# One-core hybrid decoder trunk: attention steps of the first two token tiles with scheduling priority, and the search's scratch tiles in a longer-lived pool

## The chip, the cores and the metric

The kernel runs on 1 core of one Trainium2 chip. The metric is the device time of one execution in microseconds (us), lower is better. Before the change it is 1992.75 us, the median of 3 runs (1991.83 to 1993.22).

## The reference

Two decoder layers over 512 tokens of width 1024, in float32. In each layer one projection `h @ w_in` feeds four branches: A, a gated convolution; B, sparse attention; C, a gated linear recurrence (HGRN2); M, cross-attention into 256 memory tokens. Each branch is lifted to width 1024, gated per channel, and summed; one output projection and a SwiGLU feed-forward network follow. The change touches branch B alone:

```python
def one_block(args):                       # a block of 128 queries
    qb, iqb, iwb, qpos = args
    rel = jax.nn.relu(jnp.einsum('bthd,bsd->bths', iqb, ik) * idx_scale)
    score = jnp.einsum('bths,bth->bts', rel, iwb).astype(jnp.float32)
    causal = key_pos[None, :] <= qpos[:, None]
    score = jnp.where(causal[None], score, -jnp.inf)
    _, sel = lax.top_k(score, topk)        # topk = 128 keys per query
    ...
    logits = jnp.einsum('bthd,btkd->bthk', qb, k_sel).astype(jnp.float32) * att_scale
    logits = jnp.where(valid[:, :, None, :], logits, -jnp.inf)
    p = jax.nn.softmax(logits, axis=-1).astype(v.dtype)
    return jnp.einsum('bthk,btkd->bthd', p, v_sel)
```

An indexer scores every key for every query, the 128 best keys are kept, and eight heads of 64 channels attend to these keys with one shared key and value.

## The kernel before, in words

**Weights.** Each weight chunk of 512 KB is loaded by a DMA on SyncE's queue into one of 4 buffers `w_raw`. ScalarE rounds it to a high part `w_hi` (L100, by the helper `A`), VectorE subtracts to get the low part `w_lo` (L257); there are 3 buffers of each. A product is then three matmuls per k tile: high by high (L324), high by low (L325 or L327), low by high (the other). GpSimd sums feed-forward weights by DMAs of its own meanwhile.

**The attention branch, per layer.** `select(t)` is the search for token tile t (128 queries, keys 0 to (t+1)·128): eight index heads of scores, then 16 rounds, each a MAX of the 8 largest (L1008) and a MATCH_REPLACE that strikes them out (L1009), on VectorE; last a bias is made from what was struck out (L1012, `biases[t]`). Tile 0 needs no search, its bias is the causal mask. `attend(t)` is the attention of tile t, in two halves of four heads. For each head two matmuls, the dots (L841, L842), go into a buffer `at` of PSUM, of which there are 2; one VectorE instruction (L857) reads `at`, adds the bias, writes `prob` and takes the extremum; ScalarE makes the exponential and its sum; VectorE takes the reciprocal (L860); ScalarE multiplies by it (the "copy"). TensorE transposes the four `prob` (L871) into a buffer `tr`, ScalarE copies them to `pt`, and after both halves matmuls with the values and the write to `y_b` (L890) follow.

**What stands beside it.** The searches are woven with `lift(3)`, the lift and gate of branch M. Then the pool `att` opens, and `attend` of tiles 0 to 3 is woven with `values(hv)` (the value projection of branch C, results `hv`) and with `lift(0)` (the gates and lift of branch A: products `mm`, then VectorE's gate operations L222, L665, L684, L685).

**What sets the order.** A scheduler orders the instructions of each engine by priority, which is the place in the program unless `tc.high_priority(offset=n)` moves it n forward; the weights' splits and some evictions have an offset of AHEAD = 3000. Each engine then runs its list strictly in that order. Pools hand out memory in a stack: `dsa` holds q, k, v and biases of branch B and lives through attend; `idx` is nested in it, holds the index heads' tensors, the score and the top-k scratch `m8`, and ends before the attention. A tile that takes memory of a closed pool waits for the tiles that stood there.

The functions that the change touches:

Of the kernel before, what the change touches and what calls it, by code (L numbers as in the profile page):

```python
# [12 lines left out]
F32 = mybir.dt.float32  # L13
# [8 lines left out]
P = 128  # L22
S = 512
# [18 lines left out]
NONC = -2.0e38  # L42
OFF = -1.0e30
AHEAD = 3000
EARLY = ["mmbmcmcbmmmsccbmscmbscmbsbbss", "mnmbmcmcbmmmsccbmscmbscmbsbbss"]
MM_BUFS = 3
TR_BUFS = 3
# [24 lines left out]
def hybrid_trunk(ctx: ExitStack, tc: tile.TileContext, x, mem, positions, norm_mix, w_in, conv_w,  # L72
# [20 lines left out]
    def A(dst, src, func, **kw):  # L93
        name = tables.get(func)
        if name is not None and name != table["set"]:
            load = act.preload_act_table_set(name)
            for u in table["users"]:
                tc.add_manual_dep(load.ins, u.name, order, reason="table set")
            table.update(set=name, load=load.ins, users=[])
        i = act.activation(dst, src, func, **kw)  # L100
        if name is not None:
            tc.add_manual_dep(i.ins, table["load"].name, order, reason="table set")
            table["users"].append(i.ins)
        return i
# [4 lines left out]
    def at_ps():  # L109
        return pat.tile([P, 512], F32, name="at", bufs=AT_BUFS)  # L110

    def tr_ps():
        return pat.tile([P, 512], F32, name="tr", bufs=TR_BUFS)
# [101 lines left out]
    def small(n, name="small", bufs=12):  # L215
        return consts.tile([P, 8], F32, name=name, bufs=bufs)[:, :n]
# [11 lines left out]
    class Chunk:  # L228
        def __init__(self, src, kt, n):
            self.kt, self.step = kt, min(kt, 1024 // n)  # L230
            self.parts = []
            for k in range(0, kt, self.step):
# [11 lines left out]
                else:  # L244
                    for g in range(2):
                        nc.sync.dma_start(raw.rearrange("p k (g c) -> p k g c", g=2)[:, :, g, :], src[:, k:e, g, :])
                with tc.high_priority(offset=AHEAD):
                    if len(raw_loads) == 1:
# [37 lines left out]
    def features(w, a, js, k0=0, kt=None, pss=None, made=None, late_lo=False):  # L286

        kt = w.kt if kt is None else kt
        pss = [mm_ps() for _ in js] if pss is None else pss
        runs = [(part, ks) for part in range(2) for ks, _, _ in w.parts] if late_lo else [(None, ks) for ks, _, _ in w.parts]  # L290
        for part, ks in runs:
            for j, ps in zip(js, pss):
                for k in ks:
                    last = mm3(ps, w.tile(k, j), pair(a, k0 + k), k0 + k == 0, k0 + k == kt - 1, part=part)[-1]
            if made is not None and (ks[-1] == w.kt - 1 or not late_lo):
                made.append(last)
        return pss
# [232 lines left out]
    def mem_kv(l):  # L530
# [21 lines left out]
        for t, ps in enumerate(products(0)):  # L552
            ku = sp.tile([P, 4, P], F32, name="ku_w", bufs=2)
            with tc.high_priority(offset=AHEAD):
                A(ku.rearrange("p a b -> p (a b)"), ps, AF.Copy)
# [23 lines left out]
        for t, ps in enumerate(products(512)):  # L579
            ps = ps.rearrange("p (h d) -> p h d", d=P)  # L580
            hi, lo = (kv[:, :, 1, e, t * P:(t + 1) * P] for e in range(2))
            with tc.high_priority(offset=AHEAD):
                A(hi, ps, AF.Copy, scale=mem_r[:, t:t + 1])
# [50 lines left out]
    def mixer(l, h, norms, cm):  # L634
# [19 lines left out]
        def lift(n, y, merged, last=None):  # L654
            def gates(m):
# [7 lines left out]
                for g, ps in zip(gs, features(gw, h, (0, 1), made=made, late_lo=made is not None)):  # L663
                    with tc.high_priority(offset=AHEAD):
                        dve.tensor_mul(g, ps, r_b)  # L665
# [5 lines left out]
            for m in range(0, KD, 2):  # L671
# [6 lines left out]
                for i in range(2):  # L678
                    g, pl = gs[i], pls[i]
                    with tc.high_priority(offset=AHEAD):  # L680
                        if n == 3:
# [33 lines left out]
        def conv_branch(y):  # L715
            for c2 in range(2):
                us = [gate_tile(), gate_tile()]
                w = wchunk(w_in[l][:, C_AX + c2 * 256:C_AX + (c2 + 1) * 256], KD, 256)
                for u, ps in zip(us, features(w, h, (0, 1))):
                    (dve if l or c2 else pool).memset(u[:, 0:2], 0.0)  # L720
                    with tc.high_priority(offset=AHEAD):
                        i = dve.tensor_mul(u[:, 2:], ps, r_b)
# [109 lines left out]
        with pool_("dsa") as dp:  # L832
# [8 lines left out]
                return [pe.matmul(ps, q[:, hh, s], k[0][:, :n], start=True, stop=False),  # L841
                        pe.matmul(ps, q[:, hh, s], k[1][:, :n], start=False, stop=True)]  # L842

            def attend(t, dp2, y_b):
                n = (t + 1) * P
                s = slice(t * P, (t + 1) * P)
                pts = []
                for q in range(2):
                    probs = []
                    for i in range(4):  # L850
                        ps = at_ps()[:, :n]
                        two = dots(ps, qS, kS, 4 * q + i, t, n)
                        if t == 0 and q + i // 2:
                            first_dots.extend(two)
                        p = dp2.tile([P, S], F32, name="prob", bufs=PR_BUFS)[:, :n]
                        mx, sm = small(1), small(1)
                        dve.tensor_tensor_reduce(out=p, in0=ps, in1=biases[t], scale=-1.0, scalar=-OFF * 4,  # L857
                                                 op0=OP.add, op1=OP.min, accum_out=mx)
                        A(p, p, AF.Exp, bias=mx, scale=-1.0, accum_out=sm)
                        dve.reciprocal(sm, sm)  # L860
                        copy = A(p, p, AF.Copy, scale=sm)
                        if l and t == 0 and q == 0 and i // 2:
                            first_probs.append(copy)
                        probs.append(p)
                    pt = dp2.tile([P, NT, S], F32, name="pt", bufs=PT_BUFS)
                    copied = []
                    for b in range(t + 1):
                        pp = tr_ps()
                        for e in range(2):
                            for i in range(2):  # L870
                                turn = pe.transpose(pp[:, (2 * e + i) * P:(2 * e + i + 1) * P],  # L871
                                                    probs[2 * i + e][:, b * P:(b + 1) * P], ident)
                        copied.append(A(pt[:, b, :], pp, AF.Copy))
                    pts.append(pt)
                    if q == 0:
                        yield
                pv = tr_ps()
                for q, pt in enumerate(pts):
                    c = slice(q * 2 * P, (q + 1) * 2 * P)
                    for b in range(t + 1):  # L880
                        for e in range(2):
                            i = pe.matmul(pv[e * HD:(e + 1) * HD, c], vt[:, b, :], pt[:, b, e * 2 * P:(e + 1) * 2 * P],  # L882
                                          start=b == 0, stop=b == t)
                            if q == 0 and b == 0:
                                tc.add_manual_dep(i.ins, turn.ins.name, order, reason="turns first")
                                tc.add_manual_dep(i.ins, copied[max(t - 1, 0)].ins.name, sync, reason="values together")
                pv = pv.rearrange("p (a b) -> p a b", b=P)
                hi, lo = (x[:, :, s] for x in y_b)
                A(hi, pv, AF.Copy)
                dve.tensor_sub(lo, pv, f(hi))  # L890
                yield

            with pool_("idx") as ip:
                iqS = ip.tile([P, 8, S], F32R, name="iqS")
# [95 lines left out]

                def select(t):
                    n = (t + 1) * P
                    score = ip.tile([P, S], F32, name="score", bufs=1)[:, :n]
                    for hh in range(8):
                        ps = at_ps()[:, :n]
                        dots(ps, iqS, ikS, hh, t, n)
                        rel = wide()[:, :n]
                        A(rel, ps, AF.Relu, scale=HD ** -0.5)
                        if hh == 0:
                            dve.tensor_scalar(score, rel, iw[:, t, 0:1], 0.0, op0=OP.mult, op1=OP.add)  # L1000
                        else:
                            dve.scalar_tensor_tensor(score, rel, iw[:, t, hh:hh + 1], score, op0=OP.mult,
                                                     op1=OP.add)
                    dve.copy_predicated(score[:, t * P:], future, neg.to_broadcast([P, P]))
                    yield
                    for i in range(TOPK // 8):
                        m8 = ip.tile([P, 16], F32, name="m8", bufs=2)[:, :8]
                        dve.max(m8, score)  # L1008
                        dve.match_replace(score, m8, score, REPL)  # L1009
                        if i % 4 == 3:  # L1010
                            yield
                    dve.tensor_scalar(biases[t], score, REPL, OFF, op0=OP.not_equal, op1=OP.mult)  # L1012
# [20 lines left out]
                with pool_("memat", "left") as mp:  # L1033
                    sel = chain(select(1), select(2), select(3))
                    script(EARLY[l], {"b": projections(), "c": conv_branch(y_a), "m": mem_branch(mp, y_m), "s": sel, "n": late_norm()})
                mgp = cm.enter_context(pool_("mgp", "left"))
                merged = mgp.tile([P, KD, S], F32, name="merged")
                weave(lift(3, y_m, merged), sel, R1)
            y_b = new_y()
# [644 lines left out]
```

## Time and profile before

| | |
|---|---|
| median of 3 runs | 1992.75 us (1991.83 to 1993.22) |
| profiled execution, its own time | 1991.71 us |
| its span | 1989.7 us |
| granted TensorE clock, mean | 0.994 |
| TensorE busy | 1959.2 us (98%) |
| VectorE busy | 1468.1 us (74%) |
| ScalarE busy | 1171.7 us (59%) |
| GpSimd busy | 236.1 us (12%) |

The profile is one execution. PE is TensorE's matmuls, PEld its weight loads, DVE is VectorE, ACT ScalarE, POOL GpSimd, SP SyncE. A row of a timeline gives start, length, engine, line, operation and tile, and in brackets how long the engine was idle before it and which instruction ended that. PEclk is the clock that TensorE was granted, 1.00 being full. Matmuls are pipelined: a row's length is longer than the distance to the next row, so the distance of starts is what a matmul costs.

### The profile page before, as it was taken

The page shows a single profiled execution, that of the slowest core. Times are in us where ns is not written, and L with a number is a line of the kernel's source. Part 1 is how long each engine was busy: PE and PEld are TensorE (multiplying, and loading weights), DVE is VectorE, ACT ScalarE, POOL GpSimd, SP SyncE. Part 2 cuts the span into 40 slices and gives each one's busy share as a digit, 9 for nine tenths or more (in the row PEclk, how much of TensorE's full clock was granted, in tenths as well). Part 3 has the DMA queues.
Part 4 walks back from the last instruction along what each step waited for, and adds up shares of the span by engine and source line. Part 5 has one row for each costly group of instructions (what it writes and reads, how often), then busy time and mean ns, then how long its engine had stood idle before and what let it go on. Part 6 is the DMA issues. An engine that isn't in the chain of part 4 may idle for free.

```text
span 1989.7 us, 26286 instructions
## 1 busy us (share of the span) xinstructions
PE 1959.2 (98%) x9495; PEld 1626.9 (82%) x9495; DVE 1468.1 (74%) x2569; ACT 1171.7 (59%) x1950; POOL 236.1 (12%) x288
## 2 busy tenths in 40 slices
PE   9999997999999999999999999989999999999999
PEld 8888886878888888888888888768888888888887
DVE  7865898658776677776876589975678667767777
ACT  6744563866665466645654547368567656646554
POOL 1011111111111111100011111111111111111000
PEclk9999998999999999999999999989999999999999
DMA  8677776667677888876677766666677788898664
GB/s 301 206 182 174 164 168 139 161 146 179 169 195 197 236 237 245 252 213 187 201 216 174 179 157 161 147 165 155 158 170 170 202 201 239 252 270 249 201 189 138
DMA packets 220178, 385.22 MB, mean 194 GB/s; under 512 B 13194, under 2 KB 114128, under 8 KB 219792
## 3 DMA queue, kind: packets, MB, share of 16 engines
q1 hardware_dynamic: 160960, 244.16, 39.4%
q0 software_dynamic: 52192, 132.81, 33.1%
q10 hardware_dynamic: 6896, 6.58, 1.0%
q8 instruction: 74, 1.21, 0.3%
q14 instruction: 56, 0.46, 0.1%
HBM read 368.81 MB, written 140.51 MB: 256 GB/s over the span
## 4 chain that ended last, share of the span: by engine, by line
PE 96%; DVE 3%; ACT 0%; issue 0%; DVEq 0%; ACTq 0%
PE mm L327 23%; PE mm L324 23%; PE mm L325 23%; PE at L324 4%; PE at L325 4%; PE at L327 4%; PE tr L324 2%; PE tr L327 2%; PE tr L325 2%; DVE score L1009 1%; DVE m L1008 1%; PE tr L871 1%; PE tr L882 1%; PE tr L1576 1%; PE at L841 1%; PE at L842 1%
## 5 line engine op out<-in xcount | busy, mean ns | idle before, releaser
L100 ACT ACTIVATE w_hi<-w_raw 128x1024 fp32r<-128x1024 f32 (+1 forms) x435 | 457.5, 1054 | 360.0 <-PE mm L325 121.4
L324 PE MATMUL mm<-h_hi,w_hi 128*128 128x512 f32 x960 | 377.0, 394 | 0.6 <-DVE zg L1075 0.6
L325 PE MATMUL mm<-h_lo,w_hi 128*128 128x512 f32 x960 | 376.6, 392 | 0.0
L327 PE MATMUL mm<-h_hi,w_lo 128*128 128x512 f32 x960 | 375.9, 398 | 0.0
L257 DVE TENSOR_TENSOR w_lo<-w_raw,w_hi 128x1024 fp32r<-128x1024 f32 (+1 forms) x224 | 272.1, 1217 | 111.4 <-ACT w_hi L100 108.7
L1287 DVE TENSOR_TENSOR w_lo<-w_raw,w_hi 128x1024 fp32r<-128x1024 f32 x211 | 256.4, 1218 | 130.0 <-ACT w_hi L100 129.2
L1302 POOL DMA_DIRECT2D up_sums<-in_ffn_w_up_dram x120 | 121.5, 1012 | 827.7 <-DMA up_sums<-in_ffn_w_up_dram 531.5
L327 PEld LDWEIGHTS mm<-h_hi,w_lo 128*128 128x128 f32 x960 | 183.1, 191 | 37.2 <-issue 0.2
L324 PEld LDWEIGHTS mm<-h_hi,w_hi 128*128 128x128 f32 x960 | 180.4, 188 | 36.6 <-issue 1.0
L325 PEld LDWEIGHTS mm<-h_lo,w_hi 128*128 128x128 f32 x960 | 180.4, 188 | 36.4 <-issue 0.2
L327 PE MATMUL mm<-w_hi,h_lo 128*128 128x512 f32 (+2 forms) x408 | 152.0, 373 | 0.0
L325 PE MATMUL mm<-w_lo,h_hi 128*128 128x512 f32 (+2 forms) x408 | 151.7, 372 | 0.3 <-DVE w_lo L257 0.3
L324 PE MATMUL mm<-w_hi,h_hi 128*128 128x512 f32 (+2 forms) x408 | 145.6, 372 | 0.0
L1302 POOL DMA_DIRECT2D w_sums<-in_ffn_w_down_dram x66 | 62.3, 944 | 339.7 <-DMA w_sums<-in_ffn_w_down_dram 192.2
L100 ACT ACTIVATE prob<-prob,small 128x128 f32<-128x128 f32 (+3 forms) x128 | 68.8, 554 | 49.1 <-DVE small L857 39.9
L325 PEld LDWEIGHTS mm<-w_lo,h_hi 128*128 128x128 f32 x408 | 76.8, 188 | 12.8 <-DVE w_lo L257 0.6
L324 PEld LDWEIGHTS mm<-w_hi,h_hi 128*128 128x128 f32 x408 | 76.8, 188 | 12.3 <-ACT w_hi L100 0.2
L327 PEld LDWEIGHTS mm<-w_hi,h_lo 128*128 128x128 f32 x408 | 76.8, 188 | 11.8
L325 PE MATMUL mm<-y_lo,w_hi 128*128 128x512 f32 x192 | 75.5, 393 | 0.0
L327 PE MATMUL mm<-y_hi,w_lo 128*128 128x512 f32 x192 | 75.3, 392 | 0.0
L324 PE MATMUL mm<-y_hi,w_hi 128*128 128x512 f32 x192 | 75.2, 394 | 0.0
L325 PE MATMUL mm<-w_lo,a_hi 128*128 128x512 f32 x160 | 63.2, 395 | 0.0
(496 smaller groups left out, 4219.6 us busy)
## 6 DMA issues: line engine op xcount, KB each, us to landing
w_raw<-in_w_in_dram SPq DMA_DIRECT2D x140, 512.0 KB, 4.6
up_sums<-in_ffn_w_up_dram POOLq DMA_DIRECT2D x120, 512.0 KB, 6.8
w_raw<-up_sums SPq DMA_DIRECT2D x80, 512.0 KB, 5.1
w_raw<-in_ffn_w_up_dram SPq DMA_DIRECT2D x60, 512.0 KB, 4.8
w_sums<-in_ffn_w_down_dram POOLq DMA_DIRECT2D x54, 512.0 KB, 6.3
up_sums<-up_sums POOLq DMA_DIRECT2D x40, 512.0 KB, 5.0
w_raw<-in_w_lift_dram SPq DMA_DIRECT2D x32, 512.0 KB, 4.3
w_raw<-in_ffn_w_down_dram SPq DMA_DIRECT2D x24, 512.0 KB, 5.3
```

The lines of the kernel that those rows point to most:

```text
L100: i = act.activation(dst, src, func, **kw)
L257: i2 = dve.tensor_sub(lo, raw, f(hi))
L324: made += [pe.matmul(ps, ah, bh, start=first, stop=False, skip_group_check=more), pe.matmul(ps, ah, bl, start=False, stop=False, skip_grou ...
L325: pe.matmul(ps, ah, bl, start=False, stop=False, skip_group_check=more)]
L327: made += [pe.matmul(ps, al, bh, start=False, stop=last, skip_group_check=more)]
L841: return [pe.matmul(ps, q[:, hh, s], k[0][:, :n], start=True, stop=False), pe.matmul(ps, q[:, hh, s], k[1][:, :n], start=False, stop=True)]
L842: pe.matmul(ps, q[:, hh, s], k[1][:, :n], start=False, stop=True)]
L871: turn = pe.transpose(pp[:, (2 * e + i) * P:(2 * e + i + 1) * P], probs[2 * i + e][:, b * P:(b + 1) * P], ident)
L882: i = pe.matmul(pv[e * HD:(e + 1) * HD, c], vt[:, b, :], pt[:, b, e * 2 * P:(e + 1) * 2 * P], start=b == 0, stop=b == t)
L1008: dve.max(m8, score)
L1287: two = A(hi, raw, AF.Copy), dve.tensor_sub(lo, raw, f(hi))
L1302: i = nc.gpsimd.dma_start(dst, src, **kw)
```

## The change

Two edits. The scratch tiles `score` and `m8` of the search are taken from the pool `dsa` instead of `idx`, so they live until the attention's end. And every step of `attend` (a step runs to the next `yield`: a half of the heads, or the second half with the values) is issued under a priority offset EAGER[t]: 700 for tiles 0 and 1, nothing for tiles 2 and 3. `attend` as it was is renamed `attend_steps`.

```diff
 AHEAD = 3000
+EAGER = [700, 700, 0, 0]
...
-            def attend(t, dp2, y_b):
+            def attend_steps(t, dp2, y_b):
...
+            def attend(t, dp2, y_b):
+                g = attend_steps(t, dp2, y_b)
+                while True:
+                    with tc.high_priority(offset=EAGER[t]):
+                        done = next(g, g) is g
+                    if done:
+                        return
+                    yield
+
...
-                    score = ip.tile([P, S], F32, name="score", bufs=1)[:, :n]
+                    score = dp.tile([P, S], F32, name="score", bufs=1)[:, :n]
...
-                        m8 = ip.tile([P, 16], F32, name="m8", bufs=2)[:, :8]
+                        m8 = dp.tile([P, 16], F32, name="m8", bufs=2)[:, :8]
```

All engines keep the same instructions. The orders of GpSimd and SyncE are as before; those of the other three differ only in the attention's stretch of each layer. Lines of the changed kernel stand 1 higher behind L44 and 10 higher behind L891. Three places, all in layer 0; layer 1 has moved alike.

VectorE, at the end of the search for tile 3 before the change. `m8` and `score` are the search's, `prob_3459` and `prob_3469` are the probabilities of tile 0's first two heads, `w_lo_3612`, `w_lo_3618` the low parts of the gate chunk of `lift(0)`, `w_lo_3690` that of its lift chunk:

```order
L1008 MAX m8_3090<-score_2883 128x8
L1009 MATCH_REPLACE score_2883<-m8_3090,score_2883 128x512
L1012 TENSOR_SCALAR bias3_786<-score_2883 128x512
L857 ISA prob_3459,small_3460<-at_3456,causal_bias_91 128x128
L857 ISA small_3460 128x1
L857 ISA prob_3469,small_3470<-at_3466,causal_bias_91 128x128
L857 ISA small_3470 128x1
L257 TENSOR_TENSOR w_lo_3612<-w_raw_3610,w_hi_3611 128x1024
L257 TENSOR_TENSOR w_lo_3618<-w_raw_3616,w_hi_3617 128x1024
L257 TENSOR_TENSOR w_lo_3690<-w_raw_3688,w_hi_3689 128x1024
L860 RECIPROCAL small_3461<-small_3461 128x1
```

VectorE after the change, from the second round of that search:

```order
L1018 MAX m8_2936<-score_2883 128x8
L858 ISA prob_3459,small_3460<-at_3456,causal_bias_91 128x128
L858 ISA small_3460 128x1
L1019 MATCH_REPLACE score_2883<-m8_2936,score_2883 128x512
L858 ISA prob_3469,small_3470<-at_3466,causal_bias_91 128x128
L858 ISA small_3470 128x1
L861 RECIPROCAL small_3461<-small_3461 128x1
L1018 MAX m8_2939<-score_2883 128x8
L861 RECIPROCAL small_3471<-small_3471 128x1
L1019 MATCH_REPLACE score_2883<-m8_2939,score_2883 128x512
```

The first two probabilities and their reciprocals have moved from behind round 16 to rounds 2 and 3; the three `w_lo` follow in and behind rounds 5 and 6, and further probabilities, reciprocals and gate operations stand among rounds 9 to 16.

TensorE, at the end of the value projection (`mm_3354`, `tr_3355` are its outputs for two token tiles), before the change:

```order
L324 MATMUL tr_3355<-w_hi_3347,h_hi_146 128x512
L325 MATMUL tr_3355<-w_lo_3348,h_hi_146 128x512
L327 MATMUL tr_3355<-w_hi_3347,h_lo_147 128x512
L841 MATMUL at_3456<-k_hi_780,qS_779 128x128
L842 MATMUL at_3456<-k_lo_781,qS_779 128x128
L841 MATMUL at_3466<-k_hi_780,qS_779 128x128
L842 MATMUL at_3466<-k_lo_781,qS_779 128x128
L324 MATMUL mm_3624<-h_hi_146,w_hi_3611 128x512
```

and the same dots after it:

```order
L325 MATMUL mm_3354<-w_hi_3341,h_hi_146 128x512
L842 MATMUL at_3456<-k_hi_780,qS_779 128x128
L843 MATMUL at_3456<-k_lo_781,qS_779 128x128
L326 MATMUL mm_3354<-w_lo_3342,h_hi_146 128x512
L328 MATMUL mm_3354<-w_hi_3341,h_lo_147 128x512
L842 MATMUL at_3466<-k_hi_780,qS_779 128x128
L843 MATMUL at_3466<-k_lo_781,qS_779 128x128
L325 MATMUL tr_3355<-w_hi_3341,h_hi_146 128x512
```

The two dot pairs stood behind the last matmul of the value projection, and stand 32 rows earlier, within the projection's first half chunk. The transpose of `prob_3459` has moved too, from the row in front of the L327 of the gate chunk to five rows in front of the gate chunk's first L324.

ScalarE, where the probabilities of tile 0's first heads are made, before the change:

```order
L100 ACTIVATE w_hi_3689<-w_raw_3688 128x1024
L100 ACTIVATE prob_3459,small_3461<-prob_3459,small_3460 128x128
L100 ACTIVATE prob_3469,small_3471<-prob_3469,small_3470 128x128
L100 ACTIVATE prob_3459<-prob_3459,small_3461 128x128
L100 ACTIVATE prob_3469<-prob_3469,small_3471 128x128
L100 ACTIVATE w_hi_3922<-w_raw_3921 128x1024
L100 ACTIVATE w_hi_3928<-w_raw_3927 128x1024
L100 ACTIVATE prob_3479,small_3481<-prob_3479,small_3480 128x128
```

and after it:

```order
L101 ACTIVATE prob_3469<-prob_3469,small_3471 128x128
L101 ACTIVATE hv_3324<-mm_3352,rstd_t_407 128x512
L101 ACTIVATE w_hi_3611<-w_raw_3610 128x1024
L101 ACTIVATE w_hi_3617<-w_raw_3616 128x1024
L101 ACTIVATE hv_3324<-mm_3353,rstd_t_407 128x512
L101 ACTIVATE hv_3324<-mm_3354,rstd_t_407 128x512
L101 ACTIVATE hv_3324<-tr_3355,rstd_t_407 128x512
L101 ACTIVATE w_hi_3689<-w_raw_3688 128x1024
L101 ACTIVATE w_hi_3922<-w_raw_3921 128x1024
L101 ACTIVATE w_hi_3928<-w_raw_3927 128x1024
L101 ACTIVATE prob_3479,small_3481<-prob_3479,small_3480 128x128
```

The four rows of the first two probabilities have moved ahead of the evictions `hv` and of the gate chunk's `w_hi_3611` and `w_hi_3617`; the next chunk's `w_hi_3922` and `w_hi_3928` stand, as before, ahead of the second two.

## The prediction

> **What bounds the kernel now.** I read the page first: the busy line and the chain that ended last.
>
> ```profile
> span 1989.7 us, 26286 instructions
> PE 1959.2 (98%) x9495; PEld 1626.9 (82%) x9495; DVE 1468.1 (74%) x2569; ACT 1171.7 (59%) x1950; POOL 236.1 (12%) x288
> PE 96%; DVE 3%; ACT 0%; issue 0%; DVEq 0%; ACTq 0%
> ```
>
> TensorE is idle for 1989.7 − 1959.2 = 30.5 us, and the chain spends 3% of the span on VectorE. The change adds no matmul and takes none away, so it can win only from those 30.5 us and from what follows an idle stretch. The table of TensorE's waits says where they are (total, count, longest):
>
> ```profile
> PE at L841 <- DVE small L857: 15.9, 2, 8.0
> PE tr L871 <- ACT prob L100: 6.0, 2, 3.0
> ```
>
> Two lines hold 15.9 + 6.0 = 21.9 us, two waits each, one per layer; L841 and L871 are the dots and the transposes of attend. The timeline of TensorE shows the place in layer 0 (start, length, idle before it in brackets):
>
> ```profile
> 320.16 0.22 PE L841 MATMUL at<-k_hi,qS 128*128 128x128 f32 x1
> ...
> 320.56 0.45 PE L324 MATMUL mm<-h_hi,w_hi 128*128 128x512 f32 x1
> ...
> 327.65 0.39 PE L325 MATMUL mm<-h_lo,w_hi 128*128 128x512 f32 x1
> 336.01 0.47 PE L841 MATMUL at<-k_hi,qS 128*128 128x128 f32 x1 [7.97 <-DVE small L857]
> ...
> 340.13 0.47 PE L871 MATMUL tr<-ident,prob 128*128 128x128 f32 x1 [3.01 <-ACT prob L100]
> 340.26 5.19 PE L327 MATMUL mm<-h_hi,w_lo 128*128 128x512 f32 x16
> 345.29 0.39 PE L324 MATMUL mm<-y_hi,w_hi 128*128 128x512 f32 x1
> ```
>
> and in layer 1:
>
> ```profile
> 1291.44 0.39 PE L325 MATMUL mm<-h_lo,w_hi 128*128 128x512 f32 x1
> 1299.79 0.47 PE L841 MATMUL at<-k_hi,qS 128*128 128x128 f32 x1 [7.96 <-DVE small L857]
> ...
> 1303.92 0.48 PE L871 MATMUL tr<-ident,prob 128*128 128x128 f32 x1 [3.01 <-ACT prob L100]
> 1304.05 6.18 PE L327 MATMUL mm<-h_hi,w_lo 128*128 128x512 f32 x16
> 1310.07 0.39 PE L324 MATMUL mm<-y_hi,w_hi 128*128 128x512 f32 x1
> ```
>
> The first two pairs of dots of token tile 0 are done at 320.6 and fill both `at` buffers. The second two pairs need a buffer back, which L857 on VectorE frees. The timeline of VectorE says why that comes only at 335.9:
>
> ```profile
> 311.03 0.69 DVE L1008 MAX8 m<-score 128x8 f32<-128x512 f32 x1
> ...
> 312.55 0.69 DVE L1008 MAX8 m<-score 128x8 f32<-128x512 f32 x1
> ...
> 335.32 0.43 DVE L1012 TENSOR_SCALAR bias<-score 128x512 f32<-128x512 f32 x1
> 335.66 0.28 DVE L857 CUSTOM_DVE_ANT_0 prob<-at,causal_bias 128x128 f32<-128x128 f32 x1
> ...
> 336.08 3.49 DVE L257 TENSOR_TENSOR w_lo<-w_raw,w_hi 128x1024 fp32r<-128x1024 f32 x3
> 339.49 0.22 DVE L860 RECIPROCAL small<-small 128x1 f32<-128x1 f32 x2
> ```
>
> The sixteen top-k rounds of the search for tile 3 run without a break from 311.03 to 335.3, 1.52 us a round. Behind them in VectorE's order stand the first probabilities, then three `w_lo`, then the reciprocals for which ScalarE's copy waits; hence the second wait of 3.01. Search 3 makes `bias3`, which only tile 3 needs, last of all.
>
> **The change part by part.** *The tiles moved to the longer-lived pool.* No instruction is added. The search's scratch no longer ends the index pool, so what is allocated where that pool stood need not wait for search 3; it lets the search run on while attend starts. By itself I cost it at nothing.
>
> *The priority.* VectorE, TensorE and ScalarE keep the same instructions in another order; SyncE's and GpSimd's orders are unchanged, and attend issues no DMA. At VectorE the first probability of tile 0 now stands behind round 2 of search 3 instead of round 16; at TensorE the first two pairs of dots are 32 rows earlier and the transposes stand in front of the gate chunk's first matmuls.
>
> What that returns, layer 0. The matmul interval is (327.65 − 320.56)/31 = 0.229, there being 31 rows between those two. The last L325 ends its interval at 327.88, and the rows of L324 on `y_hi` start at 345.29: 17.41 us, in which TensorE does four dots (320.56 − 320.16 = 0.40), a transpose (0.13) and 16 L327 (3.66), together 4.2. Loss 17.4 − 4.2 = 13.2. Layer 1 in the same way: 1310.07 − 1291.67 = 18.4, less 4.2: 14.2. Sum **27.4**, of which 21.9 are idle and 5.5 slow matmuls after the idle (16 L327 in 5.19 and 6.18 instead of 3.66, and dots).
>
> The slow ones show in the granted clock, in the table by windows (window, length, busy of PE, PEld, DVE, ACT, POOL, then PEclk, DMA share, GB/s):
>
> ```profile
> 311.00:320.00 9.00, 9.00 (x42) 7.44 (x41) 8.59 (x18) 2.21 (x3) 1.35 (x2) 1.00 0.52 124
> 320.00:328.00 8.00, 8.00 (x38) 6.39 (x36) 7.62 (x17) 3.16 (x4) 1.15 (x1) 1.00 0.63 100
> 328.00:336.00 8.00, 0.04 (x1) 0.00 (x0) 7.66 (x19) 0.01 (x1) 1.01 (x2) 0.80 0.36 80
> 336.00:345.30 9.30, 6.28 (x22) 5.09 (x23) 4.33 (x13) 4.42 (x13) 1.30 (x2) 0.62 0.89 233
> 345.30:355.00 9.70, 9.70 (x50) 8.12 (x49) 7.93 (x20) 8.23 (x21) 1.14 (x1) 1.00 0.95 204
> 355.00:365.00 10.00, 10.00 (x51) 8.07 (x51) 6.46 (x21) 7.66 (x21) 1.43 (x2) 1.00 0.71 190
> 365.00:375.00 10.00, 10.00 (x57) 8.02 (x54) 7.49 (x18) 9.78 (x22) 1.16 (x1) 1.00 0.58 132
> ```
>
> PEclk falls to 0.80 and 0.62 around the idle and is 1.00 elsewhere; beyond the idle, layer 0 lost 13.2 − 11.0 = 2.2 and layer 1 14.2 − 11.0 = 3.2 us. [...]
>
> *What VectorE must do in time instead.* Its first rows: round 1 ends at 312.55, round 2's MAX at 313.2, then the probabilities, while TensorE's dots are done at about 313.2: wait at most 0.2. From there I go by the order. ScalarE has `w_hi` of the gate chunk's two parts behind the four probability rows, at some 317 to 319; TensorE asks for the first at 320.7. `w_lo` of both parts stand at the two ends of round 5's MATCH_REPLACE, where I put their ends at 319.6 and 321.5; TensorE asks at 328.4. These rows set ScalarE's lengths and the place of the old copy:
>
> ```profile
> 316.87 1.05 ACT L100 ACTIVATE w_hi<-w_raw 128x1024 fp32r<-128x1024 f32 x1
> 321.52 2.00 ACT L100 ACTIVATE w_hi<-w_raw 128x1024 fp32r<-128x1024 f32 x2
> 335.99 0.40 ACT L100 ACTIVATE prob<-prob,small 128x128 f32<-128x128 f32 x1 [12.46 <-DVE small L857]
> ```
>
> New on ScalarE is that the `w_hi` of the next chunk stand ahead of tile 0's second exponentials in a stretch where TensorE still reads the buffers that they take: I put the end of the second at 329.4; the transposes of those probabilities are wanted at about 334, so the exponentials, the reciprocals and the copies have 4 us. Its weights load earlier than before, as their raw buffers come free when `w_lo` is taken out of the queue behind the search:
>
> ```profile
> w_raw<-in_w_in_dram SPq DMA_DIRECT2D x140, 512.0 KB, 4.6
> ```
>
> So TensorE ends its L327 at about 332.1 instead of 345.3.
>
> Next is the count that decides whether it can go on. VectorE from 311.03 to the probability that frees the buffer for the sixth dot pair of tile 1: 16 rounds 24.3, bias3 0.4, twelve probabilities (eight at 0.21, four at 0.42) 3.4, eight `w_lo` at 1.16 9.3, ten gate operations at 0.64 6.4, ten reciprocals at 0.11 1.1; 44.9, so 355.9, and with one `w_lo` that waits for its `w_hi` (1.05 and a little, put at 1.3) 357.2. TensorE's side: 332.1, 99 matmuls 22.7, 31 small ones at about 0.12 3.7: 358.5. Slack 1.3, the smallest that I find; the earlier ones are 2 to 4. Rows for the lengths not yet shown:
>
> ```profile
> 346.50 1.28 DVE L665 TENSOR_TENSOR gate<-mm,rstd 128x512 f32<-128x512 f32 x2
> 357.66 0.42 DVE L857 CUSTOM_DVE_ANT_0 prob<-at,bias 128x256 f32<-128x256 f32 x1
> ```
>
> As a check: VectorE's busy time from 311 to 375 is 8.59 + 7.62 + 7.66 + 4.33 + 7.93 + 6.46 + 7.49 = 50.1, and the stretch would be 64 − 13.2 = 50.8 long. It fits, but only if VectorE hardly ever waits. It is then the engine that nearly bounds. Over the whole stretch it need not be so tight, since some of the work of 355 to 375 may slip behind. I therefore leave 1 us of stall per layer in the sum (0 to 4 each).
>
> *Later stages.* GpSimd's sums of weights run at their own pace and could now be late by 13 us a layer. In layer 1 the last is issued at 1833, and their loads begin at 1936:
>
> ```profile
> 1833.04 1.13 POOL L1302 DMA_DIRECT2D w_sums<-in_ffn_w_down_dram  x1 [3.54 <-DMA w_sums<-in_ffn_w_down_dram]
> ...
> 1936.46 20.73 SPq L1388 DMA_DIRECT2D w_raw<-w_sums  x9
> ```
>
> A shift of 27 stays hidden in those 103 us. Price: nothing.
>
> Sum against the profiled execution, 1991.71 (span 1989.7 and 2.0 around it): 1991.71 − 27.4 + 2 × 1 = 1966.3. The median of the runs is 1.04 above that execution, so **1967.3**.
>
> **The rivals.** *Half of it comes back as VectorE's waits.* VectorE's order is fixed, and a reciprocal in it waits for ScalarE's exponential with top-k rounds behind it. Of the old stretch from 310 to 425 the waits table says
>
> ```profile
> DVE small L860 <- ACT prob L100: 11.3, 11, 4.7
> ```
>
> From 345.3 to 375 VectorE was busy 21.9 of 29.7 us: 74%. If it packs half-way between that and full, 87%, the 50.1 us take 57.6; 57.6 − 50.8 = 6.8 lost per layer: 1992.75 − 27.4 + 13.6 = **1979**. For it speaks that row; against it, that those rounds need nothing from any other engine and fill most gaps, and that the long waits stood where ScalarE had the whole of its work late.
>
> *Slower.* VectorE packs no better than the 74% through the whole stretch: 50.1/0.74 = 67.7 instead of 64, +3.7 per layer: **2000**. The place is the reciprocal behind each pair of probabilities; TensorE would then wait at the dots of tile 1 again and again, each time with a lowered clock. It decides below 50.1/64 = 78%. Against it: the stretch from 311 to 328 ran at 95%.
>
> *The wait only changes its name.* TensorE is released at the dots and stands as long at the next row that needs VectorE, 1992.75. The order speaks against it, since `w_lo` and probabilities have moved ahead of at least ten rounds.
>
> **How the numbers follow.** Forecast 0.71, half of it lost 0.17, slower 0.07, no change 0.05. The range's lower end, 1962, is the sum without a stall, 1965.3, and a few of the other 8.6 us of idle; the upper, 1982, holds the second case and a little. About 0.15 lie outside. A measurement of this kernel can tell 0.2%, some 4 us, from no change: faster 0.88, same 0.05, slower 0.07.
>
> **What would show it.** Right: the two lines of L841 and L871 gone from TensorE's waits, PEclk at 1.00 through both places, TensorE's idle near 8 to 11 us, L1018 and L858 alternating on VectorE from 313, VectorE over 90% busy from 311 to 357. Half right: new waits of TensorE at the dots of tile 1 on L858, or on `w_hi`. Wrong: idle of TensorE at 25 us or more, in whatever place, or lost time outside the two stretches.

## The result, and the profile after

| | before | after |
|---|---|---|
| median | 1992.97 us (4 runs, 1991.83 to 1993.22) | 1969.17 us (4 runs, 1968.80 to 1970.16) |
| ratio | | 0.9882, 95% interval 0.9865 to 0.9900 |
| profiled execution, span | 1989.7 us | 1966.6 us |
| TensorE idle in the span | 30.5 us | 10.1 us |

The change saves 23.8 us, 1.2%. The forecast was a gain of 25.4 on the median, to 1967.3; the result lies inside its range. In the profiled executions the span is 23.1 us shorter. The page of the changed kernel, its busy line and its chain:

```profile
span 1966.6 us, 26277 instructions
PE 1956.5 (99%) x9495; PEld 1623.9 (83%) x9495; DVE 1461.2 (74%) x2569; ACT 1173.0 (60%) x1950; POOL 236.4 (12%) x288
PE 99%; DVE 0%; ACT 0%; issue 0%; DVEq 0%; ACTq 0%
```

VectorE has left the chain. TensorE's idle is 1966.6 − 1956.5 = 10.1. Both old waits of TensorE, 15.9 and 6.0 us, are gone from its table of waits; two small ones are new, on ScalarE's copies `pt` of the transposes:

```profile
PE tr L872 <- ACT pt L101: 0.9, 2, 0.5
...
PE tr L883 <- ACT pt L101: 0.6, 2, 0.3
```

The stretch in layer 0, in the table by windows with the same columns as before:

```profile
311.00:320.00 9.00, 9.00 (x44) 7.46 (x43) 8.50 (x22) 5.03 (x11) 1.21 (x1) 1.00 0.55 137
320.00:328.00 8.00, 8.00 (x38) 6.62 (x37) 7.79 (x15) 3.04 (x4) 1.15 (x1) 1.00 1.00 222
328.00:336.00 8.00, 8.00 (x43) 6.67 (x42) 7.80 (x21) 4.80 (x11) 0.57 (x1) 1.00 0.61 160
336.00:345.30 9.30, 9.30 (x45) 7.71 (x44) 9.30 (x27) 7.04 (x19) 1.74 (x2) 1.00 0.69 203
345.30:355.00 9.70, 9.70 (x49) 8.05 (x48) 7.76 (x22) 6.75 (x15) 1.14 (x1) 1.00 0.79 146
```

TensorE is busy throughout and its clock stays at 1.00. VectorE, the third number, is busy 8.50 + 7.79 + 7.80 + 9.30 + 7.76 = 41.2 of 44 us, 94%. Its timeline has the first probability of tile 0 and the fourth of tile 1 here:

```profile
313.11 0.29 DVE L858 CUSTOM_DVE_ANT_0 prob<-at,causal_bias 128x128 f32<-128x128 f32 x1
...
354.56 0.42 DVE L858 CUSTOM_DVE_ANT_0 prob<-at,bias 128x256 f32<-128x256 f32 x1
```

And TensorE's timeline, where the two waits stood:

```profile
327.87 0.23 PE L842 MATMUL at<-k_hi,qS 128*128 128x128 f32 x1
...
328.26 3.87 PE L328 MATMUL mm<-h_hi,w_lo 128*128 128x512 f32 x16
331.97 0.39 PE L325 MATMUL mm<-y_hi,w_hi 128*128 128x512 f32 x1
```

The dots follow the gate chunk's matmuls without a gap and the 16 L328 take 3.87 us where they took 5.19.

Laying the two timelines of TensorE beside each other, row by row, tells where time was won and where some was given back. The starts of the same instruction (us):

| place | before | after | difference |
|---|---|---|---|
| layer 0, first matmul on `y_hi` behind the old waits | 345.29 | 331.97 | −13.3 |
| layer 0, first matmul behind tile 3's values | 444.60 | 433.65 | −10.9 |
| layer 1, first matmul on `y_hi` behind the old waits | 1310.07 | 1284.99 | −25.1 |
| layer 1, first matmul behind tile 3's values | 1409.33 | 1386.28 | −23.0 |

Before the first place the two kernels differ by 0.2. So the two places gave 13.1 and 14.1 us, and in the rest of attend 2.4 and 2.0 went back. From the end of attend to the end of the layer the difference is constant: in layer 0 10.9 us still at 974.39 of the kernel before (963.46 after), in layer 1 23.05 still at its last matmul (1984.99 and 1961.94). Two questions are left: which half of the change brought the gain, and what took 4.4 us of it back.

### The profile page after: what moved, and what is told of

It is laid out like the page before. It is cut to its first block, busy times and chain, and to the rows that moved or that the text cites. A ratio compares the mean times of both kernels' runs of the same rounds, so it can differ in the third digit from the quotient of the medians.

```text
span 1966.6 us, 26277 instructions
## 1 busy us (share of the span) xinstructions
PE 1956.5 (99%) x9495; PEld 1623.9 (83%) x9495; DVE 1461.2 (74%) x2569; ACT 1173.0 (60%) x1950; POOL 236.4 (12%) x288
## 4 chain that ended last, share of the span: by engine, by line
PE 99%; DVE 0%; ACT 0%; issue 0%; DVEq 0%; ACTq 0%
PE mm L325 24%; PE mm L326 24%; PE mm L328 24%; PE at L325 4%; PE at L326 4%; PE at L328 4%; PE tr L325 2%; PE tr L328 2%; PE tr L326 2%; PE tr L883 1%; PE at L842 1%; PE at L843 1%; PE tr L1586 1%; PE tr L872 1%; PE tr L940 0%; PE tr L809 0%
## 5 line engine op out<-in xcount | busy, mean ns | idle before, releaser
L328 PE MATMUL mm<-h_hi,w_lo 128*128 128x512 f32 x960 | 372.8, 394 | 0.0
L328 PEld LDWEIGHTS mm<-h_hi,w_lo 128*128 128x128 f32 x960 | 180.2, 188 | 36.3 <-issue 0.2
L328 PE MATMUL mm<-w_hi,h_lo 128*128 128x512 f32 (+2 forms) x408 | 152.0, 373 | 0.0
L328 PEld LDWEIGHTS mm<-w_hi,h_lo 128*128 128x128 f32 x408 | 76.8, 188 | 11.7
L328 PE MATMUL mm<-y_hi,w_lo 128*128 128x512 f32 x192 | 75.3, 392 | 0.0
```

Source lines behind the costliest of these rows:

```text
L328: made += [pe.matmul(ps, al, bh, start=False, stop=last, skip_group_check=more)]
```

## The experiments

Times are medians. "The change" is 1969.17 (ratio 0.9882); each kernel is compared with runs of the kernel before on the same chip.

### Which half of the change does it

**The pool without the priority.**

```diff
-EAGER = [700, 700, 0, 0]
+EAGER = [0, 0, 0, 0]
```

> The scratch tiles in the longer-lived pool, no priority for any tile. Theory A (the prediction's: the priority brings the gain, the pool by itself nothing): 1992 to 1994 us, TensorE's waits at the dots and transposes as before. Theory B (the pool is what lets attend start beside the search, the priority only moves it a few rounds further): the first probabilities stand behind round 6 of search 3 instead of 16, so both waits go and 18 to 24 us are gained: 1969 to 1975 us.

1973.06 against 1992.58, ratio 0.9901 (0.9886 to 0.9915). 19.5 of the 23.8 us come without any priority. The waits of 8.0 and 3.0 are gone; the first probability on VectorE:

```profile
321.76 0.27 DVE L858 CUSTOM_DVE_ANT_0 prob<-at,causal_bias 128x128 f32<-128x128 f32 x1
```

It stands in the sixth round, 8.6 us later than in the changed kernel and still 6 us ahead of the place where TensorE asks for it (327.9). Theory B holds. At the two places of the table above this kernel wins 13.1 and 14.1 us, the same as the whole change. What the priority adds, 4.3 us by the medians and 3.1 between the profiled executions, is won elsewhere in attend. One place of it shows: in layer 0 of this kernel the last thirteen transposes of tile 3 stand in a row, with 1.81 us of waits where the changed kernel has 0.79.

**The priority without the pool.**

```diff
-                    score = dp.tile([P, S], F32, name="score", bufs=1)[:, :n]
+                    score = ip.tile([P, S], F32, name="score", bufs=1)[:, :n]
...
-                        m8 = dp.tile([P, 16], F32, name="m8", bufs=2)[:, :8]
+                        m8 = ip.tile([P, 16], F32, name="m8", bufs=2)[:, :8]
```

> The priority for tiles 0 and 1, the scratch tiles still in the index pool. Theory A: 1967 to 1972 us, as the whole change. Theory B: the first probabilities still stand behind all 16 rounds, so TensorE waits 8 and 3 us in each layer as before: 1991 to 1994 us.

1994.64, ratio 1.0009 (1.0000 to 1.0018): no gain. TensorE's waits are those of before to the tenth:

```profile
PE at L842 <- DVE small L858: 15.9, 2, 8.0
PE tr L872 <- ACT prob L101: 6.0, 2, 3.0
```

All 16 rounds still stand ahead of the first probability in VectorE's order, with an offset of 700 on it. So the priority did not take it past the search; that fits an instruction that has to wait for the search's end.

**Only the score in the longer-lived pool, `m8` back in the index pool, with the priority.**

> The changed kernel with m8 back in the index pool; the score stays in the longer-lived one, the priority stays. If one tile of the search in the closed pool is enough to hold attend back (the first probabilities then stand behind all 16 rounds of search 3): 1992 to 1995 us, both waits back. If the score alone was in the way: 1968 to 1971.

1995.11, ratio 1.0014 (1.0004 to 1.0023). Even the two small tiles `m8` in the closed pool hold all of it back. The wait changes its place but not its size:

```profile
PE tr L872 <- ACT prob L101: 24.4, 2, 12.2
```

12.2 a layer instead of 8.0 + 3.0: in this kernel the prediction's third rival comes true. VectorE's order tells which tile holds attend back. With `score` and `m8` both in the closed pool (the run before this one) the first probability stands behind the bias, the last instruction that reads `score`:

```profile
335.48 0.43 DVE L1022 TENSOR_SCALAR bias<-score 128x512 f32<-128x512 f32 x1
335.82 0.28 DVE L858 CUSTOM_DVE_ANT_0 prob<-at,causal_bias 128x128 f32<-128x128 f32 x1
```

With `m8` alone there it stands ahead of the bias, right behind the last MATCH_REPLACE, the last instruction that reads `m8`:

```profile
335.03 0.28 DVE L858 CUSTOM_DVE_ANT_0 prob<-at,causal_bias 128x128 f32<-128x128 f32 x1
...
335.23 0.42 DVE L1022 TENSOR_SCALAR bias<-score 128x512 f32<-128x512 f32 x1
```

The three runs together fit one reading: attend's tiles take the memory of the closed index pool, so what is written there waits for the last use of what stood there, and as long as one of the search's tiles is among them this is the end of the search. That moving `score` alone is not enough is shown. That `score` alone would hold attend back too is read from the first of the two orders; no run moves `m8` alone. Which tile of attend lies over which of them stays open.

**The pool, and the priority for tile 0 alone.**

```diff
-EAGER = [700, 700, 0, 0]
+EAGER = [700, 0, 0, 0]
```

> The pool and the priority for tile 0 alone. If tile 1's steps have slack, as the prediction's walk has it (1 to 4 us at each dot pair): the same as the change within 1 us, 1968 to 1970. If VectorE's order in tile 1 was the tight place, new waits of TensorE at tile 1's dots, 1972 to 1976 us.

1971.12, ratio 0.9892 (0.9877 to 0.9906): 2.0 us over the change, and neither reading fits, since no new wait stands at tile 1's dots. The time goes at the end of tile 3 in layer 1, where TensorE falls 2.8 us behind the changed kernel. The scheduler has put the last thirteen transposes in a row there, while the changed kernel has seven matmuls behind the sixth. TensorE there:

```profile
1380.41 0.82 PE L872 MATMUL tr<-ident,prob 128*128 128x128 f32 x6
1382.02 0.55 PE L872 MATMUL tr<-ident,prob 128*128 128x128 f32 x3 [0.79 <-ACT prob L101]
1383.03 0.66 PE L872 MATMUL tr<-ident,prob 128*128 128x128 f32 x4 [0.47 <-ACT pt L101]
1384.01 5.35 PE L883 MATMUL tr<-pt,vt 128*64 128x256 f32 x32 [0.32 <-ACT pt L101]
```

**The pool, and the priority for all four tiles** (`EAGER = [700, 700, 700, 700]`).

> The pool and the priority for all four tiles. The changed kernel loses 2.4 us in layer 0 and 2.1 in layer 1 between the first lift and the end of tile 3's attention, where TensorE waits for ScalarE's copies of the transposes. If that is because tile 3's steps come too late, this version gains 2 to 4 us on the change: 1965 to 1967. If it is because the last transposes and their copies have no other matmuls left beside them, the same within 1 us: 1968 to 1970.

1972.18, ratio 0.9899 (0.9882 to 0.9915): 3 us slower than the change, while by both readings it should have been no slower. In layer 1 tile 3 ends here too with thirteen transposes in a row. Priority for tile 3's steps makes that end denser in small work. This pointed to the end of tile 3 as the place of the loss.

### What the waits were worth, and what came back

**The kernel before with 8 rounds instead of 16 in the search for tile 3.**

```diff
-                    for i in range(TOPK // 8):
+                    for i in range(TOPK // 8 if t < 3 else TOPK // 16):
```

> The kernel before, with 8 rounds instead of 16 in the search for tile 3 (that tile then keeps 64 keys per query instead of 128). 8 rounds of 1.52 us fewer put the first probability at 323.5 instead of 335.7 in layer 0, before TensorE asks for it at 327.9, with no change of order. If a layer's two waits and the slow matmuls behind them are worth 13.2 and 14.2 us, as the prediction's sum says, and nothing comes back: 1965 to 1967 us, and the first wait is gone. If part of it comes back wherever the waits go: 1969 to 1972.

1965.78 against 1993.24, ratio 0.9864 (0.9849 to 0.9878): 27.5 us saved, with the old order on TensorE but for one transpose and one matmul of layer 1. Its VectorE:

```profile
323.88 0.27 DVE L857 CUSTOM_DVE_ANT_0 prob<-at,causal_bias 128x128 f32<-128x128 f32 x1
...
324.29 3.49 DVE L257 TENSOR_TENSOR w_lo<-w_raw,w_hi 128x1024 fp32r<-128x1024 f32 x3
327.70 0.21 DVE L860 RECIPROCAL small<-small 128x1 f32<-128x1 f32 x2
```

The first probability comes at 323.9 and the reciprocals at 327.7, both in time. The medians give the prediction's sum, 27.4, almost to the tenth, and that is in part luck: the two profiled executions differ by 26.0 us (1991.71 and 1965.73). In their timelines the two places give 13.2 and 13.9, and 0.8 comes back just behind the first, where TensorE waits 0.20 us for a gate operation of VectorE. So the waits are worth about what the sum says, and with the old order little of it comes back.

**The changed kernel with the same 8 rounds left out.**

> The changed kernel with the same 8 rounds left out of the search for tile 3. If the 3.6 us that the change fell short of 27.4 are lost to a VectorE that is too full (the prediction's first rival, in a small dose): 1965 to 1967 us. If they are lost at the end of tile 3's attention, where TensorE waits for ScalarE's copies of the last transposes: within 1 us of the change, 1968 to 1970.

1966.97, ratio 0.9870 (0.9854 to 0.9887), 2.2 under the change. Taken alone this would speak for VectorE's fullness, but it is inconclusive: with the shorter search the scheduler ordered TensorE's attention anew, with 19 and 10 matmuls among tile 3's last thirteen transposes, where the kernel before has 18 and 12. It changes two things at once.

**Two of the last four copies on VectorE.**

```diff
-                        copied.append(A(pt[:, b, :], pp, AF.Copy))
+                        copied.append(dve.tensor_copy(pt[:, b, :], pp) if t == 3 and q == 1 and b % 2 else A(pt[:, b, :], pp, AF.Copy))
```

> The changed kernel with two of the four copies of the last transposes (second half of tile 3) on VectorE instead of ScalarE. If TensorE waits there for ScalarE's four copies in a row (2.07 us), they are done about 1 us earlier: 0.6 to 1.0 us less in each layer, 1967 to 1968. If the loss is elsewhere: 1969 as the change, or slower by VectorE's own copies.

1968.54, ratio 0.9878 (0.9863 to 0.9893): 0.6 under the change, which is not told from none; the profiled spans are equal, 1966.6. The waits of 0.3 at the values are gone and those of 0.5 at the transposes remain.

**The end of tile 3 spread out in the changed kernel.** The rows of TensorE in the kernel before and in the changed one, at the end of tile 3 in layer 0:

```profile
432.62 0.82 PE L871 MATMUL tr<-ident,prob 128*128 128x128 f32 x6
...
437.38 0.49 PE L871 MATMUL tr<-ident,prob 128*128 128x128 f32 x3
437.62 0.48 PE L324 MATMUL mm<-h_hi,w_hi 128*128 128x512 f32 x1
...
440.46 0.60 PE L871 MATMUL tr<-ident,prob 128*128 128x128 f32 x4
440.99 3.67 PE L882 MATMUL tr<-pt,vt 128*64 128x256 f32 x32
```

```profile
425.84 0.82 PE L872 MATMUL tr<-ident,prob 128*128 128x128 f32 x6
...
428.12 0.49 PE L872 MATMUL tr<-ident,prob 128*128 128x128 f32 x3
429.07 0.66 PE L872 MATMUL tr<-ident,prob 128*128 128x128 f32 x4 [0.47 <-ACT pt L101]
430.05 3.67 PE L883 MATMUL tr<-pt,vt 128*64 128x256 f32 x32 [0.32 <-ACT pt L101]
```

Before, 18 matmuls stand ahead of the three transposes and 12 behind them, and ScalarE copies beside them. After, seven stand ahead of all seven transposes and none among them, though the same matmuls exist: the scheduler has put them earlier. From 428.12 to 430.05 TensorE spends 1.93 us on seven transposes that took 0.24 (437.38 to 437.62) and 0.53 (440.46 to 440.99) in the kernel before: 1.16 us more, of which 0.79 show as waits. The edit orders three of the transposes ahead of the seven matmuls (`last_turns` are the last eight transposes of tile 3, `last_values` its matmuls with the values, `made` the matmuls of a projection of branch C that stand beside them; the lines that collect them are left out):

```diff
...
+                        if (q, nm) == (0, "zq"):
+                            tc.add_manual_dep(made[29].ins, last_turns[3].ins.name, order, reason="turns between")
+                            for late, n in ((last_turns[4:], 32), (last_values, 35)):
+                                for i in late:
+                                    tc.add_manual_dep(i.ins, made[n].ins.name, order, reason="matmuls between")
...
```

> The changed kernel with three of the last seven transposes of tile 3 ordered ahead of the seven matmuls that the scheduler put in front of them, so that ScalarE's copies run beside matmuls as in the kernel before. If the loss of 1.8 us per layer stands there: 1.0 to 1.5 us less in each layer, 1966 to 1967.5. If the loss is elsewhere: as the change, 1969.

1967.18, ratio 0.9871 (0.9856 to 0.9885): 2.0 under the change. The same end now:

```profile
426.32 1.14 PE L875 MATMUL tr<-ident,prob 128*128 128x128 f32 x9
...
428.91 0.60 PE L875 MATMUL tr<-ident,prob 128*128 128x128 f32 x4
429.44 3.67 PE L888 MATMUL tr<-pt,vt 128*64 128x256 f32 x32
```

No wait is left there, and in the timeline TensorE gains 1.1 us on the changed kernel at this place in each layer.

**The reverse, in the kernel before**: the three transposes ordered behind the twelve matmuls, nothing else moved.

> The kernel before, with the last three transposes of tile 3 ordered behind the twelve matmuls that stand between them and the last four, so that tile 3 ends with seven transposes and sixteen value matmuls in a row, as in the changed kernel; nothing else moves. If that row of small work costs 1.5 to 2 us a layer: 1996 to 1997 us and waits of TensorE for the copies of the transposes as in the changed kernel. If the changed kernel lost its 3.6 us elsewhere: 1993.

1994.47 against 1992.09, ratio 1.0012 (1.0003 to 1.0022): 2.4 slower, less than the 3 to 4 that I expected of it. The rows have the lengths and waits of the changed kernel's:

```profile
440.66 0.49 PE L874 MATMUL tr<-ident,prob 128*128 128x128 f32 x3
441.62 0.66 PE L874 MATMUL tr<-ident,prob 128*128 128x128 f32 x4 [0.47 <-ACT pt L100]
442.59 3.67 PE L887 MATMUL tr<-pt,vt 128*64 128x256 f32 x32 [0.32 <-ACT pt L100]
```

In its timeline TensorE falls behind by 1.04 us at this place in each layer. That is the price of the dense end, shown from both sides: about 1 us a layer, not 1.8.

**Two further spreads.** First the last four transposes four matmuls behind the nine, with three more ahead of the values.

> The changed kernel with tile 3's end spread further: nine transposes, four matmuls, four transposes, three matmuls, the values (the version before this had seven matmuls between nine and four, and took 1967.2 us). If ScalarE's copies are then wholly covered: 0.3 to 0.5 us a layer less than that version, 1966 to 1966.7. If the rest of the loss is not there: 1967.

1967.12, ratio 0.9873 (0.9856 to 0.9889): the same as the simpler spread. The copies were covered already. Then, besides, the priority for the first half of tile 2.

> The same, and the first half of tile 2 with the priority as well, which leaves more matmuls at tile 3's end in layer 0 (six transposes, three matmuls, three transposes, four matmuls, four transposes, three matmuls). Layer 1 is ordered as without it. If only covered copies count: as the version without it, within 0.5 us, 1966 to 1967.

1968.38, ratio 0.9879 (0.9864 to 0.9893), 1.2 slower than without it. So covered copies are not all that counts. Layer 1 did not keep its order either: in both layers two transposes have slipped between the value matmuls of tile 1. Without the added priority those sixteen matmuls stand in a row and take 1.88 us in layer 0 (378.08 to 379.96), and the two transposes 0.13 elsewhere. Here:

```profile
378.34 0.65 PE L888 MATMUL tr<-pt,vt 128*64 128x256 f32 x2
378.92 0.44 PE L875 MATMUL tr<-ident,prob 128*128 128x128 f32 x2
379.29 1.94 PE L888 MATMUL tr<-pt,vt 128*64 128x256 f32 x14
```

The eighteen take 2.82 us, to 381.16: 0.8 more, without a row in the table of waits, and layer 1 loses as much. The profiled spans differ by 1.6.

With all the rounds of the search kept, the kernels with the spread end are the fastest of these: 1967.1 and 1967.2, against 1969.2 for the change and 1993 before.

## Why the prediction was right, point by point

**The loss at the two places: right.** 13.2 and 14.2 were summed, 13.1 and 14.1 won, and the kernel with the shorter search prices the two waits, 13.2 and 13.9, with nearly the old order. The measurement agrees with the rows, which hold 2.2 and 3.2 us beyond the idle. PEclk was low there: 0.80 from 328 to 336 and 0.62 from 336 to 345.3 before, 1.00 in the same windows after; in layer 1 0.75 from 1291 to 1299.8 and 0.55 from there to 1310.1 before, 1.00 from 1266 to 1295 after.

**VectorE's walk: right, and a little pessimistic.** First probability 313.2 forecast, 313.1 measured; the gate chunk's two low parts 319.6 and 321.5 against 319.4 and 321.2; TensorE's `y_hi` 332.1 against 332.0. The fourth probability of tile 1 was put at up to 357.2 and ended at 354.9. The count of instructions was right; too high was above all the price of the sixteen rounds, 24.3 us, which took 21.7. A MAX held VectorE for 0.73 us where its own MATCH_REPLACE followed (311.03 to 311.76 before the change) and for 0.60 where other work did (344.08 to 344.68 after it). The smallest slack, put at 1.3, was 4.9: TensorE came to that dot pair at 359.8. VectorE was busy 94% from 311 to 355, where I asked for over 90%.

**The rivals that needed a worse packing: not seen.** They rested on a reciprocal that waits for ScalarE with top-k rounds queued behind. VectorE's table of waits from 310 to 425 in the changed kernel, its first and fourth row:

```profile
DVE w_lo L258 <- ACT w_hi L101: 11.6, 7, 5.1
...
DVE small L861 <- ACT prob L101: 2.6, 6, 0.7
```

The reciprocals' 11.3 have become 2.6. The longest of the other waits, 5.1 us, stands at 416, and TensorE has no wait for VectorE in attend.

**The pool "by itself at nothing": wrong.** This is the step of the reasoning that failed, though the total did not depend on it. I gave the whole 27.4 to the priority; 19.5 come from the pool alone, none from the priority alone, and 4.3 (3.1 between the profiled executions) from the priority on top. The 27.2 of the two places come from the pool alone; what the priority adds is won elsewhere. The text had even said what the pool frees, and I did not ask which of the two moved the rows that I quoted. The order of each half alone would have shown it: 16 rounds ahead of the first probability with the priority alone, 5 and the MAX of the sixth with the pool alone.

**The residual of 1 us per layer: mis-sized, and put on the wrong engine.** It was 2.4 and 2.0, and TensorE has not one wait for VectorE in attend. About 1.04 a layer is the dense end of tile 3, shown by removing it and by adding it. Another 0.7 a layer is read from the timeline at tile 0's values. No run takes it away there, but the last kernel above lost 0.8 a layer by the same move in tile 1. Before, eight matmuls with the values and two transposes take from 364.75 to 365.96, 1.2 us;

```profile
364.75 1.08 PE L882 MATMUL tr<-pt,vt 128*64 128x256 f32 x8
365.76 0.44 PE L871 MATMUL tr<-ident,prob 128*128 128x128 f32 x2
365.96 0.48 PE L325 MATMUL mm<-y_lo,w_hi 128*128 128x512 f32 x1
```

after, the transposes have slipped between them, and the same ten take from 355.84 to 357.79, 1.95 us:

```profile
355.84 0.65 PE L883 MATMUL tr<-pt,vt 128*64 128x256 f32 x2
356.42 0.44 PE L872 MATMUL tr<-ident,prob 128*128 128x128 f32 x2
356.78 1.08 PE L883 MATMUL tr<-pt,vt 128*64 128x256 f32 x6
357.79 0.39 PE L842 MATMUL at<-k_hi,qS 128*128 128x256 f32 x1
```

The table of waits has nothing there; the rows' ends are modelled, and only the starts show the loss. What is left, 2.4 − 1.8 = 0.6 in layer 0 and 0.2 in layer 1, stays open. The forecast of 1967.3 was 1.9 under the result. Against the profiled execution, 1968.8, the sum of 1966.3 was 2.5 short, and 2.4 of that is this term. That the median misses by less is luck: it stands 0.4 above the profiled execution, where the sum took over 1.04 from the kernel before.

**Later stages: right.** The difference of the two timelines does not change from the end of attend to the end of the layer (10.9 us in layer 0, 23.05 in layer 1), so neither GpSimd's sums nor the loads took anything back.

## What to carry to other kernels

Where a pool closes and its memory is taken again, the last use of even a small tile can date what comes after: with `m8` alone in the closed pool the kernel took 1995.1 us against 1992.1 before, and a priority of 700 did not get past it; move the long-running tiles out first, and only then ask what a priority adds. When a gain falls short, lay the timelines of the bounding engine side by side, same instruction by same instruction: a loss within "busy" time, here 0.7 us a layer at tile 0's values, shows there and not in the table of waits. When several edits make one change, order each alone before giving the gain to one of them.

## What I had not expected of the hardware

In the kernel with the priority for tile 0 alone the clock was low behind a row of small TensorE work with short waits too, 0.68 in the profiled execution. The end of tile 3 in layer 1 has 1.58 us of waits within some 4 us, and the 32 value matmuls behind it take 5.35 us instead of 3.67. Its table by windows (busy of TensorE is the second number, PEclk the last but two):

```profile
1380.00:1384.00 4.00, 2.43 (x16) 1.58 (x14) 0.33 (x3) 3.15 (x7) 0.19 (x1) 1.00 0.65 111
1384.00:1389.30 5.30, 5.29 (x33) 2.95 (x33) 1.62 (x3) 0.45 (x1) 1.66 (x2) 0.68 0.29 99
```

TensorE was never idle for more than 0.8 us at once, was busy 2.43 of 4 us, and then ran at a clock of 0.68. With waits of 1.81 us at the same place the value matmuls took 3.67 us in the kernel without priority (layer 0) and in that with all four tiles (layer 1), so it did not happen every time. Nor, it seems, did it in every execution of this kernel: of its four, two have spans of 1969.6 us, the profiled one among them, and two of 1968.1 and 1968.4, of which no profile was kept. What decides it no run here shows.
